# A hybrid HGRN2 and gated DeltaNet step: unread products at the start, other first transfers, one triangular inverse per head, one set of decays, eight passes of the planner

## The chip, the cores and the metric

The kernel runs on one core of a Trainium2 chip. The metric is the device time of one execution in microseconds (us), as the median of several runs. Engines are named as in the profile: PE (TensorE), PEld (its weight loads), DVE (VectorE), ACT (ScalarE), POOL (GpSimd), SP (SyncE, which here issues every DMA; SPq is its queue).

## The reference

One layer of a decoder works on 2048 prompt tokens and 8 sample tokens of width 1024, all in fp32. The mixer, cut to what matters:

```python
p = einsum('btd,de->bte', rmsnorm(x, norm_w), w_in)      # 1024 -> 4104
hq, hf, hi, hz, gq, gk, gv, gz, gb, ga = split(p)        # 8 blocks of 512; gb, ga: 4 each
# HGRN2, 4 heads of 128: S_t = diag(f_t) S_{t-1} + k_t v_t^T;  o_t = S_t^T q_t
# gated DeltaNet, 4 heads of 128; q, k, v after a causal convolution of width 4 and SiLU; q, k l2-normed
beta = sigmoid(gb);  g = -exp(a_log) * softplus(ga + dt_bias);  G = cumsum(g) in a chunk
L = exp(where(causal, G_t - G_s, -inf))
A = where(strict, (beta_t k_t . k_s) * L, 0) + I
u = solve(A, beta v) - solve(A, beta k exp(G)) S         # unit lower triangular
o = (q exp(G)) S + ((q k^T) * L) u
S = exp(G_last) S + (k exp(G_last - G))^T u
out = concat(rmsnorm(o_hgrn) silu(hz), rmsnorm(o_gdn) silu(gz)) @ w_out
y = rmsnorm(x + out, final_norm)
```

Both recurrences start from zero for the prompt and from given states for the sample tokens; the last states are outputs too.

## The kernel before

**Tiling.** The prompt is worked in two groups (g) of 1024 tokens, each of two sub-blocks (sb) of 512. For each group and each of 4 heads (h), the loop over `steps` projects eight column blocks of 128 (HI, HZ, HF, HQ for HGRN2, GK, GQ, GV, GZ for GDN). Weights and x are split into a rounded part and a rest (`wh`, `wl`, `xh`, `xl`), and `project` (L650) makes three products for each of 8 slices of the width: xh wh, xl wh, xh wl, of 512 columns, or of 256 and 264 in the sub-block that carries the 8 sample tokens too (`segs`, L641). They go to PSUM as `ps_pj` and are emptied by the `post` of that block on ACT and DVE. `out_proj` comes last (`ps_y`).

**The start.** `prep` (L564) loads rows of x (`xt`), sums their squares on ACT (`jk`), scales them by the norm weight `nwb` on DVE, and transposes them on PE (`ps_x`, L512); ACT takes `xh` out, DVE `xl`. `fetch_w` loads weights as `raw`, and ACT and POOL make `wh` and `wl`. Small inputs come beside them: `rows` (conv weights, norms), `ald` (`a_log` and `dt_bias`, broadcast), `wgr` (weights of the two gates), the conv state (`csr`).

**GDN, chunks of 128.** A head has 8 chunks in a group, four in each sub-block. `decays` (L856) makes two exponentials of differences of G for each sub-block: `la` (token t on the partitions, mask `mnA`) and `lt` (s on the partitions, mask `mnT`). `gq_after` (L882) multiplies k k^T by `la`, and k q^T by `lt`. The diagonal 32x32 blocks of A go through DRAM (`ad`) into `xa`, 32 blocks on 128 partitions. `substitute` (L920) inverts them in 31 steps of two DVE operations:

```python
SE.tensor_tensor(tm[:, :, :n], xa[:, j + 1:, j]..., ti[:, :, j:j + 1]..., op=ALU.mult)
SE.tensor_tensor(ti[:, :, j + 1:], ti[:, :, j + 1:], tm[:, :, :n], op=ALU.subtract)
```

The blocks return through `td` into `ut`, one tile per sub-block, and `inverse` (L953), once per sub-block, builds the inverse of each 128x128 matrix on PE: two rounds of a product of `la` and `ut` (`ps_v`), its copy by DVE (`v`), a product with the transposed `tn` (`ps_u`), and its copy into `ut`. `gdn_chain` (L988) then runs the recurrence over the chunks: `ps_ks`, `rr`, `ps_u`, the copy `uu` on ACT, `ps_s`, `po_g`.

**What sets the order.** No instruction is issued in the order in which the Python text makes it. `Model.record` (L68) keeps every instruction with an assumed cost, and `plan` (L111) is a list scheduler: `play` (L152) runs all of them forward through queues V, A, G, T and S (DVE, ACT, POOL, PE, SP), taking at each moment the ready instruction of lowest rank; `play_back` (L231) runs the result backward from its end and gives new ranks. After `PASSES` such rounds the order with the earliest end is fixed on each engine. On the chip every engine works through its order and waits by semaphores; SP issues its DMAs in its order. All operations of DVE, ACT, POOL and SP go through one helper and so have one line, L392; products are L505, transposes L512 (L404, L517 and L524 in the changed kernel).

Of the kernel before, what the change touches and what calls it, by code (L numbers as in the profile page):

```python
# [33 lines left out]
PASSES = 4  # L34
# [16 lines left out]
class Model:  # L51
# [59 lines left out]
    def plan(self):  # L111
# [26 lines left out]
        for _ in range(PASSES):  # L138
            t, order, start, held, end = self.play(rank, succ, pred)
# [12 lines left out]
    def play(self, rank, succ, pred):  # L152
# [9 lines left out]
        wire = 0.0  # L162
        narrow = False
# [16 lines left out]
        for _ in range(n):  # L180
# [223 lines left out]
def build(tc, x_prompt, x_sample, state_hgrn, state_gdn, state_gdn_conv, norm_w, w_in, hg_lb_logits,  # L404
# [10 lines left out]
    with ctx:  # L415
# [99 lines left out]

        def ctile(shape, name, dt=F32):
            return const.tile(shape, dt, name=name)  # L517
# [123 lines left out]
        def segs(g, sb, part=None):  # L641
            if g == 0 and sb == 0:
# [30 lines left out]
        def gates(g, xs, gt_):  # L673
# [4 lines left out]
            for sb in range(NSB):  # L678
# [13 lines left out]
                n5 = 5 if (g == 0 and sb == 0) else 4  # L692
# [11 lines left out]
        def gates_post(g, gt, out):  # L704
# [45 lines left out]
            A.activation(eG, Gc, AF.Exp)  # L750
            out.update(beta=beta, Gc=Gc, eG=eG)
# [80 lines left out]
        def gk_after(g, h, sb, gt):  # L832
            cs = slice(sb * 4, sb * 4 + 4)

            def run(u):
# [9 lines left out]
                yield  # L845
                br = small.tile([P, 4], F32, tag="br", bufs=6, name="br")
                V.tensor_tensor(br, rk, gt["beta"][:, h, cs], op=ALU.mult)
                gam = small.tile([P, 4], F32, tag="gam", bufs=6, name="gam")
                V.tensor_tensor(gam, br, rk, op=ALU.mult)
                nge = small.tile([P, 4], F32, tag="nge", bufs=6, name="nge")  # L850
                V.scalar_tensor_tensor(nge, in0=gam, scalar=-1.0, in1=gt["eG"][:, h, cs], op0=ALU.mult, op1=ALU.mult)
                V.tensor_scalar(br, br, 0.5, None, op0=ALU.mult)
                u["br"], u["nge"], u["gam"] = br, nge, gam
            return run

        def decays(g, h, sb, gt, u, prev):  # L856
# [11 lines left out]
            for key, after, mask in (("la", "ut", mnA), ("lt", "done", mnT)):  # L868
                yield from until(lambda: after in prev)
                lx = keep.tile([P, 4, P], F32, tag=key, name=key)  # L870
                for c in range(4):
                    gcol = gt["Gc"][:, h, sb * 4 + c:sb * 4 + c + 1]
                    V.scalar_tensor_tensor(lx[:, c], in0=gb4[:, c], scalar=gcol, in1=mask, op0=ALU.subtract, op1=ALU.min, reverse0=(key == "la"))
                    yield
                A.activation(lx, lx, AF.Exp)
                u[key] = lx
# [5 lines left out]
        def gq_after(sb, U):  # L882
            def run(u):
# [9 lines left out]
                la, lt, gam = u["la"], u["lt"], u["gam"]  # L893
                for c2 in range(2):
# [6 lines left out]
                    for c in range(2):  # L901
                        cc = 2 * c2 + c
                        V.scalar_tensor_tensor(la[:, cc], in0=pk[:, c, 0], scalar=gam[:, cc:cc + 1], in1=la[:, cc], op0=ALU.mult, op1=ALU.mult)
                    V.tensor_tensor(lt[:, 2 * c2:2 * c2 + 2], pk[:, :, 1], lt[:, 2 * c2:2 * c2 + 2], op=ALU.mult)
                for b in range(4):
                    Q.dma_start(U["ad"][b, sb * 4:sb * 4 + 4].rearrange("c t s -> t c s"),
# [13 lines left out]
        def substitute(U):  # L920
# [3 lines left out]
            for cg in range(4):  # L924
                Q.dma_start(xa[32 * cg:32 * cg + 32], U["ad"].rearrange("b c t s -> (b c) t s"))
# [27 lines left out]
        def inverse(u, sb):  # L953
            la, ut = u["la"], u["ut0"]
            v1, v2 = v12[sb]
            yield from hold()
            tn = btile([P, 4, P], "tn", F32)
            V.transpose(tn.rearrange("p c k -> p (c k)"), ut.rearrange("p c k -> p (c k)"))
            yield from ready(la, ut, slot=CH)
            pv = ch.tile([P, 4, 32], F32, tag="ch", name="ps_v1")  # L960
            for c in range(4):
                for q in (0, 64):
                    mm(pv[q:q + 32, c], lhsT=la[:, c, q:q + 32], rhs=ut[:, c, q + 32:q + 64], start=True, stop=True)
            for q in (0, 64):
                V.tensor_copy(v1[q:q + 32], pv[q:q + 32])
            yield from ready(v1, tn, slot=CH)
            pu = ch.tile([P, 4, 32], F32, tag="ch", name="ps_u1")
# [863 lines left out]
```

## Time and profile before

| | us |
|---|---|
| median of 3 runs | 1274.28 (1273.73 to 1276.13) |
| the profiled execution | 1279.08 |
| its span in the profile | 1277.3 |
| PE busy | 1220.3 |
| PEld, beside PE | 1056.3 |
| DVE busy | 950.4 |
| ACT busy | 519.1 |
| POOL busy | 306.3 |

The profile shows one execution. Its views are: the page with busy times per engine; windows, which give the busy time of each engine and the granted TensorE clock (PEclk, 1.00 is 2.4 GHz) in a stretch; the timeline, with each instruction's start, its duration, and in brackets the idle time of the engine before it and what ended that; waits, grouped by what the engine waited for; and lines, groups of like instructions with busy time, mean duration in ns, and idle time before them. Products are pipelined, so the duration of one is longer than the distance to the next.

### The profile page before, as it was taken

The numbers are of one execution on the slowest core, as the hardware profiler recorded it, in microseconds if no ns is written. First come the engines' busy times: TensorE is split into PE (matmuls) and PEld (weight loads), VectorE is DVE, ScalarE is ACT, GpSimd is POOL, SyncE is SP. The second block draws the span as 40 slices with busy tenths as digits, with TensorE's granted clock in tenths as the row PEclk, the third lists the DMA queues.
The fourth block names the chain that finished last, engine by engine and source line by source line (L and its number), as shares of the span: only waits on it lengthen the run. The fifth ranks groups of instructions, "written<-read, shape, count | busy, mean of one in ns | idle before, by whom it ended". The sixth has DMA issues, their size and how long they took to land.

```text
span 1277.3 us, 21956 instructions
## 1 busy us (share of the span) xinstructions
PE 1220.3 (96%) x7943; PEld 1056.3 (83%) x7943; DVE 950.4 (74%) x2419; ACT 519.1 (41%) x1533; POOL 306.3 (24%) x304
## 2 busy tenths in 40 slices
PE   3999999999999999989999999999999999999997
PEld 3988898988898889987788878888887887877785
DVE  4467897689876986888788987896788677954433
ACT  5435523643264325653365326423622464222221
POOL 5221321332232322322224213221322220001000
PEclk9999999999999999999999999999999999999998
DMA  5222532332333321334144432221332216442442
GB/s 177 66 50 85 80 41 58 71 100 64 79 93 86 92 58 42 87 108 111 34 118 57 65 68 69 70 56 30 80 76 49 68 49 202 129 144 83 144 144 82
DMA packets 144053, 107.52 MB, mean 84 GB/s; under 512 B 26122, under 2 KB 126792, under 8 KB 143928
## 3 DMA queue, kind: packets, MB, share of 16 engines
q1 hardware_dynamic: 143936, 106.02, 32.8%
q8 instruction: 65, 1.06, 0.3%
q14 instruction: 52, 0.43, 0.1%
HBM read 82.23 MB, written 23.91 MB: 83 GB/s over the span
## 4 chain that ended last, share of the span: by engine, by line
PE 69%; DVE 15%; DMA 9%; SPq 3%; issue 2%; ACT 1%; POOL 0%; POOLq 0%; DVEq 0%; ACTq 0%
PE ps_pj L505 35%; PE ps_y L505 14%; DVE tm L392 4%; DVE ti L392 4%; SPq L392 3%; PE ps_u L505 2%; PE po_h L505 2%; PE po_g L505 2%; PE ps_kq L505 2%; DMA ut<-td 2%; DMA xt<-in_x_prompt_dram 1%; DVE E L392 1%; PE ps_g L505 1%; PE ps_ks L505 1%; PE ps_hu L505 1%
## 5 line engine op out<-in xcount | busy, mean ns | idle before, releaser
L505 PE MATMUL ps_pj<-xh,wh 128*128 128x512 f32 (+2 forms) x1328 | 469.8, 354 | 7.9 <-ACT pre L392 2.7
L505 PE MATMUL ps_pj<-xh,wl 128*128 128x512 f32 (+2 forms) x1328 | 466.2, 351 | 0.0
L505 PE MATMUL ps_pj<-xl,wh 128*128 128x512 f32 (+2 forms) x1328 | 465.2, 351 | 0.2 <-DVE xl L392 0.2
L505 PEld LDWEIGHTS ps_pj<-xh,wh 128*128 128x128 f32 x1328 | 253.4, 191 | 34.8 <-ACT pre L392 3.3
L505 PEld LDWEIGHTS ps_pj<-xl,wh 128*128 128x128 f32 x1328 | 253.5, 191 | 24.2 <-DVE xl L392 0.5
L505 PEld LDWEIGHTS ps_pj<-xh,wl 128*128 128x128 f32 x1328 | 253.4, 191 | 24.3
L392 POOL TENSOR_TENSOR wl<-raw,wh 128x512 fp32r<-128x512 f32 x128 | 172.9, 1352 | 359.6 <-ACT wh L392 319.9
L392 ACT ACTIVATE wh<-raw 128x512 fp32r<-128x512 f32 x128 | 80.5, 629 | 158.4 <-PE ps_pj L505 111.3
L392 DVE TENSOR_TENSOR tm<-xa,ti 128x248 f32<-128x248 f32 (+30 forms) x248 | 107.5, 434 | 14.6 <-DMA xa<-ad 9.4
L505 PE MATMUL ps_y<-woh,oh 128*128 128x512 f32 x256 | 101.4, 400 | 4.9 <-ACT oh L392 3.0
L505 PE MATMUL ps_y<-woh,ol 128*128 128x512 f32 x256 | 101.0, 396 | 0.0
L505 PE MATMUL ps_y<-wol,oh 128*128 128x512 f32 x256 | 100.4, 394 | 0.0
L392 DVE TENSOR_TENSOR ti<-ti,tm 128x248 f32<-128x248 f32 (+30 forms) x248 | 90.4, 365 | 7.5
L392 ACT ACTIVATE jk<-xt 128x512 bf16<-128x512 f32 (+2 forms) x54 | 40.0, 740 | 121.9 <-DVE xt L392 88.2
L392 POOL TENSOR_TENSOR rso<-sso,mhalf 128x4 f32<-128x4 f32 x32 | 35.8, 1119 | 115.7 <-DVE sso L392 111.5
L505 PEld LDWEIGHTS ps_y<-woh,oh 128*128 128x128 f32 x256 | 48.5, 190 | 15.1 <-ACT oh L392 3.5
L392 POOL TENSOR_TENSOR frs<-fss,mhalf 128x1 f32<-128x1 f32 (+1 forms) x17 | 9.5, 557 | 198.4 <-DVE fss L392 180.9
L505 PEld LDWEIGHTS ps_y<-woh,ol 128*128 128x128 f32 x256 | 48.4, 189 | 10.3 <-DVE ol L392 0.4
L505 PEld LDWEIGHTS ps_y<-wol,oh 128*128 128x128 f32 x256 | 48.6, 190 | 9.4
L392 DVE TENSOR_TENSOR xt<-ps_y,xt 128x512 f32<-128x512 f32 (+1 forms) x34 | 23.4, 688 | 39.4 <-PE ps_y L505 38.0
L392 ACT ACTIVATE s_hg<-s_hg,e 128x128 f32<-128x128 f32 x80 | 32.0, 400 | 43.0 <-DVE s_hg L392 32.3
L392 DVE SCALAR_TENSOR_TENSOR s_gd<-s_gd,el,ps_s 128x128 f32<-128x128 f32 x64 | 22.1, 346 | 30.8 <-PE ps_s L505 30.3
(290 smaller groups left out, 2169.5 us busy)
## 6 DMA issues: line engine op xcount, KB each, us to landing
raw<-in_w_in_dram SPq DMA_DIRECT2D x128, 256.0 KB
xt<-in_x_prompt_dram SPq DMA_DIRECT2D x30, 512.0 KB
og_d<-sz SPq DMA_DIRECT2D x32, 256.0 KB
og<-og_d SPq DMA_DIRECT2D x32, 256.0 KB
out_dram<-xt SPq DMA_DIRECT2D x15, 512.0 KB
gb<-gate_r SPq DMA_DIRECT2D x16, 256.0 KB
out_dram<-S SPq DMA_DIRECT2D x8, 512.0 KB
xa<-ad SPq DMA_DIRECT2D x32, 128.0 KB
```

Source lines behind the costliest of these rows:

```text
L392: r = fn(*args, **kw)
L505: r = T.matmul(out, lhsT=lhsT, rhs=rhs, start=start, stop=stop)
```

## The change

It has these parts. **Start:** `warm` writes 60 products of the identity with itself (256 columns, bf16) into `po_w`, which nothing reads. The rows of the sample tokens move from sub-block 0 to sub-block 1 (`segs`, `gates`, the decode steps), so that the first sub-block is all prompt and its projections have 512 columns from step to step; the gate weights, the conv state of the samples and its copy are loaded at step 6. **One set of decays:** `la` has no mask and no exponential of its own; it is k k^T times `lt`, so A is held transposed with its column factor `gam` applied to the result, as the scale of `uu`. `eG` changes its sign once. **Joint inverses:** `ut` holds 8 chunks, `inverse` works on all of a head's group at once, and `xa` is read along its rows. **Planner:** 8 rounds in place of 4; after the first, a DMA is not put earlier than 30 us (`AHEAD`) before the rank that the backward run gave it, and (`LANES`) a DMA may not be issued before the end of the eighth one before it.

```diff
-PASSES = 4
+PASSES = 8
+WARM = 60
+AHEAD = 30.0
+LANES = 8
...
             if not left[i]:
-                heapq.heappush(soon[recs[i][0]], (0.0, i))
+                if timed and recs[i][0] == "S":
+                    ready[i] = max(0.0, rank[i] - AHEAD)
+                heapq.heappush(soon[recs[i][0]], (ready[i], i))
...
                 wire += 0.8 * late
+                lanes.append(end)
+                if len(lanes) >= LANES:
+                    clock[k] = max(clock[k], lanes[-LANES])
...
+                if timed and recs[j][0] == "S":
+                    ready[j] = max(ready[j], rank[j] - AHEAD)
...
+        def warm(n):
+
+            o = po.tile([P, 512], F32, tag="po", bufs=2, name="po_w")
+            one = ident.bitcast(BF16)
+            for _ in range(n):
+                r = T.matmul(o[:, 0:2 * P], lhsT=one[:, 0:P], rhs=one, start=True, stop=True)
+                m.queue("T", r)
+                m.record("T", r, (0.2, 0.17, False), [o], [ident])
...
+        warm(WARM)
...
-            if g == 0 and sb == 0:
+            if g == 0 and sb == NSB - 1:
                 s = [(0, 256, 0), (256, 256, NS)]
...
             A.activation(eG, Gc, AF.Exp)
+            V.tensor_scalar(eG, eG, -1.0, None, op0=ALU.mult)
...
-            for key, after, mask in (("la", "ut", mnA), ("lt", "done", mnT)):
...
+            lt = keep.tile([P, 4, P], F32, tag="lt", name="lt")
+            for c in range(4):
+                gcol = gt["Gc"][:, h, sb * 4 + c:sb * 4 + c + 1]
+                V.scalar_tensor_tensor(lt[:, c], in0=gb4[:, c], scalar=gcol, in1=mnT, op0=ALU.subtract, op1=ALU.min)
+                yield
+            A.activation(lt, lt, AF.Exp)
...
-                        V.scalar_tensor_tensor(la[:, cc], in0=pk[:, c, 0], scalar=gam[:, cc:cc + 1], in1=la[:, cc], op0=ALU.mult, op1=ALU.mult)
+                        V.scalar_tensor_tensor(la[:, cc], in0=pk[:, c, 0], scalar=gam[:, cc:cc + 1], in1=lt[:, cc], op0=ALU.mult, op1=ALU.mult)
...
-                SE.tensor_tensor(tm[:, :, :n], xa[:, j + 1:, j].unsqueeze(1).broadcast_to(sh),
+                SE.tensor_tensor(tm[:, :, :n], xa[:, j, j + 1:].unsqueeze(1).broadcast_to(sh),
...
-            for sb in range(NSB):
-                ut = keep.tile([P, 4, P], F32, tag="ut", name="ut")
-                G.memset(ut, 0.0)
-                for b in range(4):
-                    Q.dma_start(ut[32 * b:32 * b + 32, :, 32 * b:32 * b + 32],
-                                      td[b, sb * 4:sb * 4 + 4].rearrange("c s t -> s c t"))
-                U[sb]["ut0"] = ut
-            for sb in range(NSB):
-                start(inverse(U[sb], sb), 0)
...
+            ut = keep.tile([P, 8, P], F32, tag="ut", bufs=1, name="ut")
+            G.memset(ut, 0.0)
+            for b in range(4):
+                Q.dma_start(ut[32 * b:32 * b + 32, :, 32 * b:32 * b + 32], td[b].rearrange("c s t -> s c t"))
+            start(inverse(U, ut), 0)
+
+        def inverse(U, ut):
...
+            tn = btile([P, 8, 64], "tn", F32)
+            tq = dec.tile([P, 8, 32], F32, tag="tm", name="tq")
+            V.transpose(tn, ut[:, :, 0:64])
+            V.transpose(tq, ut[:, :, 64:96])
+            yield from ready(U[1]["la"], tn, tq, slot=CH)
+            pv = ch.tile([P, 8, 32], F32, tag="ch", name="ps_v1")
+            for c in range(8):
+                mm(pv[0:32, c], lhsT=la(c)[:, 32:64], rhs=tn[:, c, 0:32], start=True, stop=True)
+                mm(pv[64:96, c], lhsT=la(c)[:, 96:128], rhs=tq[:, c], start=True, stop=True)
...
-                    A.copy(uu, p2)
+                    A.activation(uu, p2, AF.Copy, scale=u["gam"][:, c:c + 1])
...
-        open_x(xs, 0, x_all, 512 + NS)
-        open_x(xs, 1, x_all)
-        first = x_rows(0) + [(0, 4, x_sample.rearrange("b t d -> (b t) d"))] + x_rows(512)
+        open_x(xs, 0, x_all)
+        open_x(xs, 1, x_all, 512 + NS)
+        first = x_rows(0) + x_rows(512) + [(1, 4, x_sample.rearrange("b t d -> (b t) d"))]
...
+            if i == 6:
+                start(sample_state())
+                start(gate_weights())
+                Q.dma_start(o_conv_s[0, :, 0:2], state_gdn_conv[0, :, 1:3])
```

**Order on SP at the start.** Before (`xt` rows of x, `nwb` the norm weight, `raw` weights):

```order
L392 DMA xt<-in_x_prompt_dram 128x1024
L392 DMA nwb<-in_norm_w_dram 128x1024
L392 DMA xt<-in_x_prompt_dram 128x1024 x2
L392 DMA raw<-in_w_in_dram 128x4x128 x2
L392 DMA xt<-in_x_prompt_dram 128x512 x2
L392 DMA xt<-in_x_sample_dram 8x512
L392 DMA rows<-in_conv_w_dram 48x128
L392 DMA rows<-in_hg_lb_logits_dram 8x128
L392 DMA rows<-in_hg_out_norm_dram 1x128
L392 DMA rows<-in_gdn_out_norm_dram 1x128
L392 DMA xt<-in_x_sample_dram 8x512
L392 DMA out_dram<-in_state_gdn_conv_dram 8x3072
```

After:

```order
L404 DMA xt<-in_x_prompt_dram 128x1024 x2
L404 DMA nwb<-in_norm_w_dram 128x1024
L404 DMA raw<-in_w_in_dram 128x4x128 x2
L404 DMA xt<-in_x_prompt_dram 128x1024
L404 DMA xt<-in_x_prompt_dram 128x512 x3
L404 DMA rows<-in_conv_w_dram 48x128
...
L404 DMA xt<-in_x_prompt_dram 128x512
L404 DMA xt<-in_x_prompt_dram 128x1024
L404 DMA raw<-in_w_in_dram 128x4x128
L404 DMA xt<-in_x_prompt_dram 128x1024
L404 DMA raw<-in_w_in_dram 128x4x128
L404 DMA xt<-in_x_sample_dram 8x512 x2
```

A second tile of x goes ahead of `nwb`; the sample rows (8x512) stand behind the next weights, where they stood on both sides of `rows`; the copy of the conv state (`out_dram`) and, further down before, `wgr` and `ald` are no longer among the first.

**Order on ACT at the start**, from its first operations; `jk` sums squares, `xh` takes transposed rows out of PSUM. Before:

```order
L392 ACTIVATE xh<-ps_x 128x4x128 x2
L392 ACTIVATE jk,ss<-xt 8x512 x2
L392 COPY cols<-ps_rows 128x58
L392 ACTIVATE e_287<-e_287 128x8
L392 ACTIVATE xh<-ps_x 128x4x128
L392 ACTIVATE nea<-ald 128x4
L392 ACTIVATE xh<-ps_x 128x4x128
L392 COPY vc<-ps_pj 128x256
L392 ACTIVATE xh<-ps_x 128x4x128
```

After:

```order
L404 ACTIVATE wh<-raw 128x512
L404 ACTIVATE xh<-ps_x 128x4x128
L404 ACTIVATE jk,ss<-xt 128x1024
L404 ACTIVATE jk,ss<-xt 128x512 x2
L404 ACTIVATE xh<-ps_x 128x4x128
L404 ACTIVATE jk,ss<-xt 128x512
L404 COPY cols<-ps_rows 128x58
L404 ACTIVATE jk,ss<-xt 128x512
L404 ACTIVATE jk,ss<-xt 128x1024
```

The exponential `nea`, which needs `ald`, stands between two evictions before; after, it comes behind step 6. Row 1's second `xh` now stands behind the squares of the next rows. On PE, 37 of the 60 unread products stand ahead of the first transposes; the other 23 stand in groups of 1 to 5 between the first transposes and products.

**Order on PE in the first inverse.** Before, the first round (`ps_v`, one tile for each sub-block) and the second (64x64):

```order
L505 MATMUL ps_sc<-E,kp 128x128 x2
L505 MATMUL ps_v_2389<-ut,la 32x32 x8
L505 MATMUL ps_v_2415<-ut,la 32x32 x8
L505 MATMUL ps_sc<-E,kp 128x128 x2
L505 MATMUL ps_pj<-xh,wl 128x512
L505 MATMUL ps_pj<-xh,wh 128x512
L505 MATMUL ps_pj<-xl,wh 128x512
L505 MATMUL ps_u_2449<-v_706,tn 32x32 x2
L505 MATMUL ps_u_2449<-tn,v_706 32x32
...
L505 MATMUL ps_v_2493<-ut,la 64x64 x4
```

After, the second round of the joint inverse, with projections between:

```order
L517 MATMUL ps_sc<-E,kp 128x128 x3
L517 MATMUL ps_v_2484<-tn,la 64x64 x8
L517 MATMUL ps_pj<-xh,wl 128x256
L517 MATMUL ps_pj<-xh,wh 128x256
L517 MATMUL ps_pj<-xl,wh 128x256
L517 MATMUL ps_pj<-xh,wl 128x256
L517 MATMUL ps_pj<-xh,wh 128x256
L517 MATMUL ps_u_2502<-ut,v_759 64x64
L517 MATMUL ps_pj<-xl,wh 128x256
L517 MATMUL ps_u_2502<-ut,v_759 64x64 x7
```

Each round has the products of all 8 chunks in one group, and between one round and the next stand projections.

## Rows read from the trace of the kernel before

**Rows 1.** The page: span, and busy time of each engine.

```profile
span 1277.3 us, 21956 instructions
...
PE 1220.3 (96%) x7943; PEld 1056.3 (83%) x7943; DVE 950.4 (74%) x2419; ACT 519.1 (41%) x1533; POOL 306.3 (24%) x304
```

**Rows 2.** Windows: length, busy of PE PEld DVE ACT POOL, clock, DMA share, GB/s.

```profile
0.00:20.00 20.00, 6.11 (x25) 5.17 (x26) 8.80 (x25) 10.74 (x22) 12.83 (x30) 1.00 0.63 189
20.00:40.00 20.00, 13.85 (x100) 13.48 (x99) 12.43 (x26) 10.64 (x25) 6.78 (x12) 0.83 0.53 157
1268.00:1277.28 9.28, 0.00 (x0) 0.00 (x0) 2.40 (x5) 0.72 (x2) 0.55 (x1) 0.65 0.18 64
```

**Rows 3.** Timeline of PE, 0 to 42 us: start, duration, instruction, [idle before].

```profile
7.97 1.97 PE L512 MATMUL ps_x<-ident,xt 128*128 128x128 f32 x8 [7.97 <-DVE xt L392]
...
20.23 0.41 PE L505 MATMUL ps_pj<-xh,wl 128*128 128x256 f32 x1
...
21.84 0.27 PE L505 MATMUL ps_pj<-xh,wl 128*128 128x256 f32 x1
...
29.79 0.59 PE L512 MATMUL ps_x<-ident,xt 8*128 8x8 f32 x4 [4.58 <-DVE xt L392]
```

**Rows 4.** Timeline of SP's queue, 0 to 36 us.

```profile
10.99 0.22 SPq L392 DMA_DIRECT2D rows<-in_gdn_out_norm_dram  x1
15.50 0.27 SPq L392 DMA_DIRECT2D xt<-in_x_sample_dram  x1
...
17.95 0.43 SPq L392 DMA_DIRECT2D wgr<-in_w_in_dram  x1
...
23.22 1.43 SPq L392 DMA_DIRECT2D raw<-in_w_in_dram  x2
```

**Rows 5.** Timeline of ACT, 14 to 34 us.

```profile
26.31 0.20 ACT L392 ACTIVATE nea<-ald 128x4 f32<-128x4 f32 x1 [3.00 <-DMA ald<-in_gdn_a_log_dram]
```

**Rows 6.** Waits of PE: us in total, times, longest us.

```profile
PE ps_v L505 <- DMA ut<-td: 7.7, 9, 2.6
...
PE ps_pj L505 <- ACT pre L392: 2.7, 3, 1.2
...
PE ps_pj L505 <- DVE szs L392: 2.3, 1, 2.3
...
PE ps_pj L505 <- ACT vc L392: 1.7, 1, 1.7
PE ps_u L505 <- DVE v L392: 1.6, 2, 0.9
```

**Rows 7.** Timelines of SP's queue and of PE, near 200 us.

```profile
195.60 3.64 SPq L392 DMA_DIRECT2D ut<-td  x8
...
199.66 0.25 PE L505 MATMUL ps_v<-ut,la 128*32 128x32 f32 x2 [0.43 <-DMA ut<-td]
201.97 0.44 PE L505 MATMUL ps_v<-ut,la 128*32 128x32 f32 x14 [2.06 <-DMA ut<-td]
```

**Rows 8.** Windows of PE: length, busy, clock, DMA share, GB/s.

```profile
417.00:421.00 4.00, 3.93 (x19) 0.57 0.29 75
...
601.00:609.00 8.00, 6.61 (x52) 0.57 0.12 21
```

**Rows 9.** Lines of DVE: count, busy us, mean ns, idle before.

```profile
L392 DVE TENSOR_TENSOR tm<-xa,ti 128x248 f32<-128x248 f32 (+30 forms) x248 | 107.5, 434 | 14.6 <-DMA xa<-ad 9.4
L392 DVE TENSOR_TENSOR ti<-ti,tm 128x248 f32<-128x248 f32 (+30 forms) x248 | 90.4, 365 | 7.5
...
L392 DVE SCALAR_TENSOR_TENSOR la<-gb,Gc,mnA 128x128 f32<-128x128 f32 x64 | 19.7, 342 | 0.0
```

**Rows 10.** Lines of ACT: count, busy us, mean ns, idle before.

```profile
L392 ACT ACTIVATE q<-pre,cols 128x512 f32<-128x512 f32 x16 | 11.5, 721 | 0.3
...
L392 ACT ACTIVATE th<-q 128x512 f32<-128x512 f32 x16 | 10.0, 624 | 2.6 <-DVE q L392 2.4
L392 ACT ACTIVATE la<-la 128x512 f32<-128x512 f32 x16 | 10.0, 625 | 10.0 <-DVE la L392 5.6 <-PE ps_hu L505 4.4
```

More of the change, by code (lines that the diff above doesn't have):

```diff
@@ L137, in plan @@
         best = None
-        for _ in range(PASSES):
-            t, order, start, held, end = self.play(rank, succ, pred)
+        for k in range(PASSES):
+            t, order, start, held, end = self.play(rank, succ, pred, k > 0)
             if best is None or t < best[0]:
@@ L691, in gates @@
                 pt = mid.tile([P, 5, 16], F32, tag="mid", name="ps_gt")
-                n5 = 5 if (g == 0 and sb == 0) else 4
+                n5 = 5 if (g == 0 and sb == NSB - 1) else 4
                 for c in range(n5):
@@ L845, in run @@
                 yield
+                gam = small.tile([P, 4], F32, tag="gam", bufs=6, name="gam")
+                V.tensor_tensor(gam, rk, gt["beta"][:, h, cs], op=ALU.mult)
+                V.tensor_tensor(gam, gam, rk, op=ALU.mult)
                 br = small.tile([P, 4], F32, tag="br", bufs=6, name="br")
[L847 to L853, printed above, removed]
+                V.scalar_tensor_tensor(br, in0=ss, scalar=0.5, in1=rk, op0=ALU.mult, op1=ALU.mult)
+                u["br"], u["nge"], u["gam"] = br, gt["eG"][:, h, cs], gam
             return run
@@ L867, in decays @@
             u["ek"] = ek
-            for key, after, mask in (("la", "ut", mnA), ("lt", "done", mnT)):
[L869 to L876, printed above, removed]
+            yield from until(lambda: "done" in prev)
+            lt = keep.tile([P, 4, P], F32, tag="lt", name="lt")
[4 more added lines that the diff above has]
+            A.activation(lt, lt, AF.Exp)
+            u["lt"] = lt
             A.activation(gb, gb, AF.Exp)
@@ L892, in run @@
                 k2, q2 = r4(u[1]), r4(u[0])
-                la, lt, gam = u["la"], u["lt"], u["gam"]
+                yield from until(lambda: "ut" in prev)
+                la = u["la"] = keep.tile([P, 4, P], F32, tag="la", name="la")
+                lt, gam = u["lt"], u["gam"]
                 for c2 in range(2):
@@ L950, in substitute @@
-            for sb in range(NSB):
-                start(inverse(U[sb], sb), 0)
-        def inverse(u, sb):
-            la, ut = u["la"], u["ut0"]
-            v1, v2 = v12[sb]
-            yield from hold()
[L957 to L961, printed above, removed]
-                for q in (0, 64):
[L963 to L967, printed above, removed]
-            for c in range(4):
-                for q in (0, 64):
-                    mm(pu[q:q + 32, c], lhsT=tn[:, c, q:q + 32], rhs=v1[:, c], start=True, stop=True)
-                mm(pu[32:64, c], lhsT=v1[:, c], rhs=tn[:, c, 0:32], start=True, stop=True)
+            ut = keep.tile([P, 8, P], F32, tag="ut", bufs=1, name="ut")
@@ L972, in inverse @@
             for q in (0, 64):
                 V.tensor_scalar(ut[q:q + 32, :, q + 32:q + 64], pu[q:q + 32], -1.0, None, op0=ALU.mult)
-            V.tensor_scalar(tn[32:64, :, 0:32], pu[32:64], -1.0, None, op0=ALU.mult)
-            yield from ready(ut, slot=CH)
+            yield from ready(tn, slot=CH)
             pv2 = ch.tile([P, 4, 64], F32, tag="ch", name="ps_v2")
-            for c in range(4):
-                mm(pv2[:64, c], lhsT=la[:, c, 0:64], rhs=ut[:, c, 64:128], start=True, stop=True)
@@ new lines, in inverse @@
+            opened[0] -= 1
+            for q in range(2):
+                V.tensor_copy(v2[64:128, q::2], pv2[64 * q:64 * q + 64])
+            yield from ready(v2, ut, slot=CH)
+            pu2 = ch.tile([P, 4, 64], F32, tag="ch", name="ps_u2")
+            for c in range(8):
+                q = 64 * (c % 2)
+                mm(pu2[q:q + 64, c // 2], lhsT=v2[:, c], rhs=ut[:, c, 64:128], start=True, stop=True)
+            for q in range(2):
+                V.tensor_scalar(ut[0:64, q::2, 64:128], pu2[64 * q:64 * q + 64], -1.0, None, op0=ALU.mult)
@@ L988, in gdn_chain @@
+            for sb in range(NSB):
+                U[sb]["ut"] = ut[:, 4 * sb:4 * sb + 4]
         def gdn_chain(g, h, U, gt):
@@ L1176, in hgrn_chain @@
             if g == 0:
[L1177 removed]
+                start(one_at_a_time(decode_hgrn(h, U[NSB - 1])))
             if g == NG - 1:
```

51 lines of the change are left out of this document (25 added, 26 removed).

## Prediction

> **What bounds the kernel now.** I read the page first. TensorE is busy for 1220.3 of 1277.3 us, 96% [rows 1]; VectorE with 950.4 comes next. So TensorE sets the time, and the change adds 60 small products to it and takes none away: only the 57 us in which it stands idle, and the stretches at a lower clock, can be won. The windows say where the idle time lies [rows 2]: 20 - 6.11 and 20 - 13.85, 20.0 us, in the first 40; 9.3 after the last product, at 1268, which the change leaves alone; the rest, 57.0 - 20.0 - 9.3 = 27.6, is scattered over the 1228 us between.
>
> The timeline of the start shows three holes [rows 3]: nothing runs before 7.97; a first block of projections starts only at 18 (the 256-column product at 20.23 takes 0.41 us, the one at 21.84 takes 0.27: the clock is at 1.2 GHz until about 21.4, and at 2.4 after the engine has been busy since 18); then PE waits until 29.79 and the clock falls once more. SP's and ACT's timelines give the causes [rows 4, 5]: SP stands from 11 until 15.50 behind small loads, the gate weights at 17.95 go out ahead of rows that PE needs, the second block of weights is asked for only at 23.22, and ACT evicts a transposed tile after 26.31 because `nea`, ahead of it, waits 3.00 us for the 16-byte broadcasts of `ald`.
>
> For the rest I read the waits of PE [rows 6]: the inverse of GDN costs 7.7 (blocks that come back from DRAM) and 1.6; projections that wait for ACT or DVE to empty a PSUM buffer cost 2.7, 2.3 and 1.7. After some of these waits the granted clock, as a mean of the stretch, is 0.57, so near its lower level, for a few us [rows 8]: 4 x 0.43 = 1.7 us lost at 417, 8 x 0.43 = 3.4 at 601, and stretches of 4 us like the first at 202, 557 and 1076, so 10.2 in all.
>
> **The change, part by part.** The sum is made against the profiled execution, 1279.1 us (span 1277.3), which lies 4.8 over the median of 1274.3.
>
> *Start.* SP now asks for two rows of x, then the norm weight, the first weights and the other rows; sample rows, gate weights, `ald` and the conv state go behind. The hole before 29.79 (4.58 us) goes, as the three things ahead of it are gone; what is late next is the first block's second half, since ACT evicts row 1's last tile only after it has squared rows 2 and 3. The norm weight lands one load of 512 KB later, so the first transpose comes up to 1.2 us later than 7.97 (the two loads issued before it in [rows 3] are the nearest guide, an estimate). The 60 products on the identity lie where PE waits: 37 ahead of the first transpose, hidden behind the 7.97 us in which there is no data; were they not hidden, the 23 behind it would cost 23 x 256 columns at 2.4 GHz, 2.5. They should have the clock at 2.4 GHz when real work comes: 17 products and a dozen transposes ran at the lower clock in the stretches from 18 to 21.4 and from 31.7 to 35, at 0.14 us each (0.41 - 0.27) for a product, so 3 at the most. Upper bound: 20.0 - 8.0 - 1.2 + 3 = 14. Lower bound: 4.6 - 1.2 - 2.5, so about 1. I take **8**: the hole (4.6) and the clock (3) are nearly sure, and what SP gains between 11 and 15.50 pays for the later norm weight.
>
> *Inverses.* Now one inverse serves eight chunks. Of 56 products per head none goes; of the loads of `ut` 4 of 8 go. Eight issues took 3.64 us on SP, and PE began the first half at 199.66 and the second, after another wait of 2.06, at 201.97 [rows 7]: the second half waited for the later four issues. With four issues all blocks land with the first half, so the waits of second halves (2.06, and 0.9 of 1.6) go. The waits of first halves come from a substitution that ends later than planned. `tm<-xa,ti` takes 434 ns and `ti<-ti,tm` of the same sizes 365 [rows 9]; the planner books both alike. After the change `xa` is read along its row instead of down its column. If the 69 ns are the stride, 248 x 69 = 17.1 us of VectorE go, 2.1 per head, about as long as PE's waits there. So of 7.7 + 1.6 and 1.7 + 3.4 of clock (202 and 601), 14.4 in all, I take **10**. Bounds: 14 and nothing, for the joint inverse must be waited for as a whole.
>
> Two statements of the Trainium skill part here. VectorE: DVE Perf Modes, section "The TRN2 errata", gives an fp32 tensor_tensor of N elements (N + 151)/0.96 ns, with no term for a stride; by it `tm` would cost what `ti` costs already, its 69 ns would be something else and would stay, and this term would be near 5. SBUF — State Buffer, section "Door 1", says that a read pays when it leaves a 16-byte line, which the column read does at each element; by it the term is the 10 above. The two rows here differ, which speaks for the second.
>
> *Full buffers.* 64 `la<-gb` (342 ns, 19.7 us) leave VectorE [rows 9], 16 exponentials of `la` (10.0 us) leave ScalarE, and the smaller evictions of the inverse are halved in number. In exchange `uu` takes a column as scale: `q<-pre,cols` with one takes 721 ns, `th<-q` of the same size without one 624 [rows 10], so 64 x 0.097 = 6.2 us more on ScalarE, 41% busy; per chunk of the recurrence that is 0.1 us, hidden while PE has projections to run, and worth 6.2 if it had none. VectorE falls by some 19.7 + 17.1 + 5, to about 908. The waits for PSUM buffers are 2.7 + 2.3 + 1.7, with 1.7 + 1.7 of clock behind the two longest: 10.1. I take **5**. Bounds: 10 won, or 6 lost, because the order is new everywhere and new places can be planned too tight.
>
> *Nothing.* Sample rows move to the second sub-block, `eG` changes sign once, `br` and `nge` lose a few [128 x 4] operations: all on engines that aren't the bound. The wait at the output projection is not touched.
>
> Sum: 8 + 10 + 5 = 23; 1279.1 - 23 = 1256.1 for such an execution, and 4.8 less, **1251 us**, for the median.
>
> **The rivals.** *Only the start* is won: the order of some 4000 instructions is drawn anew, and new waits replace the old ones in number. For it: 27.6 us over 1228 is already little, and the planner knows neither contention nor late loads. Against: two causes above go whatever the order. 1274.3 - 8 = 1266.
>
> *All of it*: 12 + 14 + 10 = 36, so 1238. For it: the planner now counts eight loads in flight, which is what SP's stops between 11 and 15.50 look like. Against: it needs every place to be right.
>
> *Slower*: the joint inverse is waited for as a whole, at every head. Now half the recurrence can go on while the other half is inverted; afterwards nothing of the head can. If PE comes to it with no projections left, it pays what it paid at 601: 2.6 idle and 3.4 of clock, 6 us. At eight heads that is 48 in place of the 14.4 paid now: 1274.3 - 8 - 14.4 + 48 = 1300. It decides from the fourth head on (24 > 14.4 + 8), so 1276 to 1300. Against: projections stand between the rounds of the new inverse, as they did before.
>
> *The change doesn't do what it says*: the identity products and the new first transfers only fill time in which PE must wait for x in any case, and the order's new waits cost the rest. Then 1274.
>
> **How the numbers follow.** Forecast 0.52, with a range of its own from 1243 to 1259; only the start 0.20; all of it 0.13; slower 0.09; no change 0.06. The range of 8 in 10 takes in the first two and most of the third: 1234 to 1270. A measurement of this kernel can tell 0.2%, 2.5 us, from nothing. Faster by more: 0.52 + 0.20 + 0.13 = 0.85; within it 0.06; slower 0.09.
>
> **What would show it.** Right: TensorE idle for about 12 us of real work in the first 40 instead of 20.0; a granted clock of 1.0 from about 8 us on; no hole near 25 to 30; `tm` at the mean of `ti`; waits for `ut` under 4 us in all; fewer than three stretches at 0.57 after 40. Wrong: `tm` as slow as before, waits of over 2 us at one inverse after another, or a longer list of projections waiting for ACT. If TensorE's idle time after 40 stays near 27 us, only the start was won.

## The result

The changed kernel takes 1251.84 us (median of 4 runs, 1249.11 to 1256.26) against 1274.01 (4 runs): a ratio of 0.9843 [0.9814, 0.9873], 20 us (16 to 24). Ratios are given as they stand on record, with a 95% interval; they differ a little from the quotient of two medians (here 0.9826, 22 us). Measured once more beside the experiments it is 0.986 [0.9834, 0.9886]. The forecast was 1251, with a range from 1234 to 1270. The kernel before lay at 1269 to 1271 in the later comparisons, so the experiments are compared by their ratios to it; 0.001 of ratio is 1.27 us, and 0.985, between its two measurements, stands for the changed kernel.

The two profiled executions, 1279.1 and 1249.1, are 30 us apart, as the first lay 4.8 over its median and the second 2.7 under: their traces show where time went, and not how much the change is worth.

The page of the changed kernel, to be held against [rows 1]:

```profile
span 1247.3 us, 21811 instructions
...
PE 1209.9 (97%) x8003; PEld 1045.9 (84%) x8003; DVE 901.7 (72%) x2301; ACT 516.8 (41%) x1517; POOL 302.8 (24%) x292
```

TensorE is the bound as before, idle for 37 us in place of 57, while 60 products were added. VectorE lost 49 us.

The windows of the start (length, busy time of PE, PEld, DVE, ACT, POOL, clock, DMA share, GB/s), against [rows 2]:

```profile
0.00:20.00 20.00, 12.65 (x82) 10.44 (x82) 8.87 (x29) 10.77 (x23) 13.17 (x31) 0.89 0.65 217
20.00:40.00 20.00, 19.24 (x150) 17.96 (x149) 15.14 (x26) 13.28 (x30) 7.39 (x7) 0.94 0.37 111
```

TensorE stands idle for 8.1 us in place of 20.0, but unread products fill a part of that. The timeline of PE shows which, against [rows 3]:

```profile
1.58 6.05 PE L533 MATMUL po_w<-ident 128*128 128x256 bf16 x37 [1.58 <-POOL ident masks.py:199]
8.59 1.09 PE L524 MATMUL ps_x<-ident,xt 128*128 128x128 f32 x8 [0.95 <-DVE xt L404]
...
11.48 0.71 PE L533 MATMUL po_w<-ident 128*128 128x256 bf16 x5
17.00 0.33 PE L524 MATMUL ps_rows<-ident,rows 58*128 58x58 f32 x1 [4.82 <-DMA rows<-in_conv_w_dram]
...
17.85 0.42 PE L517 MATMUL ps_pj<-xh,wl 128*128 128x256 f32 x1
...
23.32 0.28 PE L517 MATMUL ps_pj<-xl,wh 128*128 128x256 f32 x1
```

The hole before 29.79 is gone. The long one is now at 17: `ps_rows` waits 4.82 us for the small loads, for which it waited 2.61 before, at about the same time:

```profile
17.49 0.33 PE L512 MATMUL ps_rows<-ident,rows 58*128 58x58 f32 x1 [2.61 <-DMA rows<-in_conv_w_dram]
```

The first eight transposes take 1.09 us, where they took 1.97 [rows 3], so the unread products did bring them the higher clock. But the product at 17.85 takes 0.42 us and that at 23.32 0.28: after 4.82 us without work the clock is at its lower level again, although 37 unread products had kept the engine busy. SP's timeline gives the cause of the wait, against [rows 4]:

```profile
6.91 2.68 SPq L404 DMA_DIRECT2D rows<-in_conv_w_dram  x1
...
13.58 0.22 SPq L404 DMA_DIRECT2D rows<-in_hg_out_norm_dram  x1
```

The first small load holds SP for 2.68 us. The last goes out only at 13.58, as SP waits 3.2 us before it for weights (`raw`) to land. Its stop before 15.50 in [rows 4], 4.3 us, ended by the profile with a landing of `raw` too, where the prediction put it down to the small loads. Projections and transposes started by 40 us, by the groups of that stretch (count, then busy us and mean ns), before and after:

```profile
L512 PE MATMUL ps_x<-ident,xt 128*128 128x128 f32 (+1 forms) x52 | 10.5, 348 | 17.1 <-DVE xt L392 17.1
L505 PE MATMUL ps_pj<-xh,wh 128*128 128x256 f32 (+1 forms) x24 | 8.1, 341 | 0.3 <-ACT xh L392 0.3
L505 PE MATMUL ps_pj<-xl,wh 128*128 128x256 f32 (+1 forms) x24 | 7.6, 327 | 0.0
L505 PE MATMUL ps_pj<-xh,wl 128*128 128x256 f32 (+1 forms) x22 | 7.0, 319 | 0.0
```

```profile
L517 PE MATMUL ps_pj<-xh,wl 128*128 128x256 f32 x33 | 10.3, 315 | 0.7 <-POOL wl L404 0.6
L517 PE MATMUL ps_pj<-xh,wh 128*128 128x256 f32 x33 | 10.3, 317 | 0.0
L517 PE MATMUL ps_pj<-xl,wh 128*128 128x256 f32 x33 | 10.2, 311 | 0.0
L524 PE MATMUL ps_x<-ident,xt 128*128 128x128 f32 (+1 forms) x66 | 9.8, 280 | 1.0 <-DVE xt L404 1.0
```

That is 99 projections against 70, and 70 transposes (these 66 and 4 of `vc`) against 52. Products start 0.12 us apart, transposes 0.11: 3.5 + 2.0, so **5.5 us** are won at the start of this execution. That of after_again, with 98 and 61, gives 4.4.

PE's waits, against [rows 6] (us in total, times, longest):

```profile
PE ps_rows L524 <- DMA rows<-in_conv_w_dram: 4.8, 1, 4.8
PE ps_v L517 <- DVE tn L404: 3.9, 2, 3.3
PE ps_pj L517 <- ACT pre L404: 2.9, 2, 2.1
PE ps_pj L517 <- DVE szs L404: 2.5, 1, 2.5
PE ps_u L517 <- DVE v L404: 2.4, 2, 1.7
...
PE ps_pj L517 <- DVE sz L404: 1.3, 1, 1.3
```

At the inverse 6.3 us are left of 9.3 (11.1 with the two small groups of `ps_v` that the prediction left out). The waits for full buffers have other places and the same sum: 2.9 + 2.5 + 1.3, 6.7, as 2.7 + 2.3 + 1.7 before. After 40 us two stretches run at a low clock, where there were five [rows 8] (length, busy, clock):

```profile
326.00:330.00 4.00, 4.00 (x51) 0.57 0.15 35
532.00:540.00 8.00, 6.79 (x43) 0.79 0.63 205
```

That is 4 x 0.43 + 8 x 0.21 = 3.4 us lost, where it was 10.2. (The execution of after_again has three such stretches, 5.1 us.)

The lines of VectorE's substitution, against [rows 9]:

```profile
L404 DVE TENSOR_TENSOR ti<-ti,tm 128x248 f32<-128x248 f32 (+30 forms) x248 | 90.7, 366 | 7.5
L404 DVE TENSOR_TENSOR tm<-xa,ti 128x248 f32<-128x248 f32 (+30 forms) x248 | 85.3, 344 | 16.9 <-DMA xa<-ad 9.0 <-DMA wor<-in_w_out_dram 2.8
```

`tm` takes 344 ns, 90 less than before, and `ti` 366 as ever. On ScalarE the scaled copy costs 101 ns more, before and after:

```profile
L392 ACT COPY uu<-ps_u 128x128 f32<-128x128 f32 x64 | 16.9, 264 | 55.7 <-PE ps_u L505 55.1
```

```profile
L404 ACT ACTIVATE uu<-ps_u,gam 128x128 f32<-128x128 f32 x64 | 23.4, 365 | 59.7 <-PE ps_u L517 59.3
```

One thing the prediction had not looked at: the second round of an inverse, 64 columns per product, on PE's timeline, where each of these fp32 products has two entries. Before, the 4 chunks of a sub-block, 8 entries:

```profile
207.45 0.68 PE L505 MATMUL ps_v<-ut,la 128*64 128x64 f32 x8
```

After, 8 chunks, 16 entries:

```profile
193.65 0.69 PE L517 MATMUL ps_v<-tn,la 128*64 128x64 f32 x16 [0.59 <-DVE tn L404]
```

16 entries take as long as 8 did. The second of two chunks writes partitions 64 to 127 of PSUM, where all wrote 0 to 63 before.

### The profile page after: what moved, and what is told of

It reads as the page before. It is cut to its first block, busy times and chain, and to the rows that moved or that the text cites. A ratio compares the mean times of both kernels' runs of the same rounds, so it can differ in the third digit from the quotient of the medians.

```text
span 1247.3 us, 21811 instructions
## 1 busy us (share of the span) xinstructions
PE 1209.9 (97%) x8003; PEld 1045.9 (84%) x8003; DVE 901.7 (72%) x2301; ACT 516.8 (41%) x1517; POOL 302.8 (24%) x292
## 4 chain that ended last, share of the span: by engine, by line
PE 81%; DMA 8%; DVE 6%; ACT 1%; SPq 1%; issue 1%; POOL 1%; POOLq 0%; DVEq 0%; ACTq 0%
PE ps_pj L517 47%; PE ps_y L517 14%; PE po_g L517 2%; PE po_h L517 2%; PE ps_kq L517 2%; PE ps_u L517 2%; DMA xt<-in_x_prompt_dram 1%; SPq L404 1%; DMA wor<-in_w_out_dram 1%; PE ps_s L517 1%; PE ps_g L517 1%; DMA raw<-in_w_in_dram 1%; PE ps_hu L517 1%; PE ps_ks L517 1%; PE ps_o L524 1%
## 5 line engine op out<-in xcount | busy, mean ns | idle before, releaser
L404 POOL TENSOR_TENSOR wl<-raw,wh 128x512 fp32r<-128x512 f32 x128 | 170.0, 1331 | 368.9 <-ACT wh L404 302.2
L404 DVE TENSOR_TENSOR tm<-xa,ti 128x248 f32<-128x248 f32 (+30 forms) x248 | 85.3, 344 | 16.9 <-DMA xa<-ad 9.0
L517 PEld LDWEIGHTS ps_y<-wol,oh 128*128 128x128 f32 x256 | 48.2, 188 | 10.2 <-DVE wol L404 0.8
L404 ACT ACTIVATE uu<-ps_u,gam 128x128 f32<-128x128 f32 x64 | 23.4, 365 | 59.7 <-PE ps_u L517 59.3
```

The source lines that it names most:

```text
L404: r = fn(*args, **kw)
L517: r = T.matmul(out, lhsT=lhsT, rhs=rhs, start=start, stop=stop)
```

## The experiments

Twelve kernels, each against the kernel before on the same chip:

| run | median us | kernel before beside it | ratio | 95% interval |
|---|---|---|---|---|
| after_again | 1253.58 | 1270.16 | 0.9860 | 0.9834 to 0.9886 |
| a_onehalf | 1259.85 | 1270.92 | 0.9898 | 0.9870 to 0.9927 |
| a_tinywarm | 1254.87 | 1270.92 | 0.9875 | 0.9851 to 0.9899 |
| a_column | 1263.43 | 1270.92 | 0.9935 | 0.9910 to 0.9959 |
| b_row | 1266.10 | 1270.92 | 0.9955 | 0.9934 to 0.9976 |
| a_neither | 1268.02 | 1269.17 | 0.9976 | 0.9958 to 0.9995 |
| a_column_told | 1249.55 | 1269.17 | 0.9847 | 0.9825 to 0.9869 |
| a_split | 1249.74 | 1270.16 | 0.9843 | 0.9815 to 0.9871 |
| a_decays | 1248.12 | 1270.16 | 0.9814 | 0.9789 to 0.9839 |
| b_start | 1283.89 | 1270.16 | 1.0109 | 1.0078 to 1.0140 |
| a_plan4 | 1256.60 | 1269.17 | 0.9909 | 0.9889 to 0.9929 |
| a_fit | 1248.12 | 1269.17 | 0.9840 | 0.9823 to 0.9858 |

Names with a_ are edits of the changed kernel, with b_ of the kernel before. In the first five of the table that aren't after_again every instruction stands where it stood, so that only what was edited differs; the others have an order drawn anew.

**after_again**, without an edit.

> The changed kernel once more, as it is, as the base for the runs beside it: a ratio of 0.982 to 0.986 to the kernel before by every theory.

0.986, at the upper end of what was expected; the two measurements of the changed kernel agree.

**a_onehalf**

```diff
...
-                q = 64 * (c % 2)
-                mm(pv2[q:q + 64, c // 2], lhsT=la(c)[:, 64:128], rhs=tn[:, c], start=True, stop=True)
+                mm(pv2[0:64, c], lhsT=la(c)[:, 64:128], rhs=tn[:, c], start=True, stop=True)
...
-                mm(pu2[q:q + 64, c // 2], lhsT=v2[:, c], rhs=ut[:, c, 64:128], start=True, stop=True)
+                mm(pu2[0:64, c], lhsT=v2[:, c], rhs=ut[:, c, 64:128], start=True, stop=True)
...
```

> The changed kernel with one thing undone: the products of the second round (ps_v2, ps_u2, 64 columns) all write partitions 0 to 63, as in the kernel before; the order on every engine is the same, and so is the number of copies. Theory A (a gain that my prediction left out: chunks that take turns between the two halves of the partitions run side by side, 31 and 35 ns apart in the changed kernel's trace against 63 and 65 before): the distance goes back to about 64 ns, 256 x 31 = 8 us, so about 1260. Rival B (the distance hangs on the new order around them, not on the partitions): the distance stays near 33 ns and the time near 1252.

The 16 entries of the first inverse on PE's timeline:

```profile
197.27 1.15 PE L517 MATMUL ps_v<-tn,la 128*64 128x64 f32 x16 [0.59 <-DVE tn L404]
```

1.15 us where the changed kernel takes 0.69. With 16 such groups that is 16 x 0.46 = 7.4 us, and the ratio says 0.0048, 6 us. The interval overlaps that of after_again a little, but the same edit made on a_column (a_neither, below) costs 0.0041, 5 us, too. Theory A: chunks that write to different halves run side by side.

**a_column** and **b_row**: one line, each way.

```diff
-                SE.tensor_tensor(tm[:, :, :n], xa[:, j, j + 1:].unsqueeze(1).broadcast_to(sh),
+                SE.tensor_tensor(tm[:, :, :n], xa[:, j + 1:, j].unsqueeze(1).broadcast_to(sh),
```

> The changed kernel with xa read down its column, as before; every engine's order is the same. It reads the other triangle of the blocks, so its values differ, not its work. Theory A (the stride costs VectorE time, and substitutions that end late are what PE waits for): tm goes from 344 ns back to about 434, 248 x 90 = 22 us of VectorE, 2.8 per head; PE's waits at the inverse grow by 1 to 2.8 at each of several heads, 1257 to 1264. Rival B (slack in the new order covers it): tm slows down, the time stays within 2 of 1252. Rival C (a VectorE operation has no term for a stride): tm stays at 344.

> The kernel before with xa read along its row; every engine's order is the same. It reads the other triangle of the blocks, so its values differ, not its work. Theory A (late substitutions): tm goes from 434 to about 344 ns, PE's wait for ut falls from 7.7 to about 3, and with the clock behind two of these waits the time falls by 5 to 9, 1265 to 1269. Rival B (the wait is that for DMA issues behind one another, whatever the substitution takes): tm falls, the waits and the time of 1274 stay.

In a_column `tm` is back at the old duration, and 0.0085, 11 us, are lost:

```profile
L404 DVE TENSOR_TENSOR tm<-xa,ti 128x248 f32<-128x248 f32 (+30 forms) x248 | 110.6, 446 | 16.8 <-DMA xa<-ad 11.7
```

But not where theory A had it. PE's waits in a_column:

```profile
PE ps_v L517 <- DVE tn L404: 4.1, 2, 3.5
PE ps_pj L517 <- ACT vc L404: 3.2, 1, 3.2
PE ps_u L517 <- DVE v L404: 2.7, 2, 2.1
...
PE ps_pj L517 <- ACT thf L404: 1.9, 2, 1.2
PE ps_kp L524 <- DVE kp L404: 1.7, 1, 1.7
```

The inverse waits 4.1 and 2.7, as with the row read (3.9 and 2.4). What is new are projections and transposes that wait for ScalarE and VectorE (`vc` 3.2, `thf` 1.9, `kp` 1.7). One place shows the chain, on ScalarE and PE:

```profile
544.50 1.06 ACT L404 ACTIVATE jk<-xt 128x1024 bf16<-128x1024 f32 x1 [3.26 <-DMA xt<-in_x_prompt_dram]
...
545.55 0.35 ACT L404 COPY vc<-ps_pj 128x256 f32<-128x256 f32 x1
```

```profile
545.96 0.58 PE L517 MATMUL ps_pj<-xh,wh 128*128 128x256 f32 x1 [3.18 <-ACT vc L404]
```

ScalarE stands 3.26 us for rows of x that landed late, the copy `vc` is queued behind them, and PE waits for its buffer; the clock then falls (0.58 us for the next product). Between the two profiled executions, 14.4 us apart, PE is idle for 7.9 us more (45.3 against 37.4) and busy for 6.5 more with the same products (1216.4 against 1209.9), at a mean granted clock of 0.986 against 0.992: the clock behind the waits costs nearly as much as the waits. Why that load is late wasn't followed; the substitution shares VectorE with the steps that free the tiles of x, which would explain it and isn't shown. In b_row `tm` falls from 434 to 326 ns, PE's wait for `ut` from 7.7 to 5.3 only, and 0.0045, 6 us, are won.

**a_neither**: both edits of a_onehalf and a_column.

> The changed kernel with both of a_onehalf and a_column: second round in one half of the partitions, xa read down its column (the other triangle, so its values differ, not its work); every engine's order is the same. Theory A (these two made nearly the whole gain, and start, joint inverse, single decays and planner come to nothing together; 7 and 12 add up): 1268 to 1273, a ratio of 0.998 or more to the kernel before. Rival B (both fill the same slack): 1262 to 1265, about 0.993. Rival C of the prediction (start and order are worth 13): 1260.

0.9976 [0.9958, 0.9995]: the two edits take 0.0126, 16 us, of the 19 away, nearly their sum (6 + 11). All else in the change is worth 1 to 5 us together, though the start is in it whole (99 projections and 68 transposes by 40 us).

**a_column_told**: a_column, and the planner books 0.10 us more for `tm`.

```diff
+                m.more = 0.1
                 SE.tensor_tensor(tm[:, :, :n], xa[:, j + 1:, j].unsqueeze(1).broadcast_to(sh),
...
+                m.more = 0.0
...
-        return 0.155 + 0.06 * scal + (0.00047 if fast else 0.00105) * n, 0.0, not psum and op != "transpose"
+        return self._m.more + 0.155 + 0.06 * scal + (0.00047 if fast else 0.00105) * n, 0.0, not psum and op != "transpose"
```

> a_column with the planner told that tm takes 0.10 us longer than it books; the order is drawn anew. Theory A (what cost 12 in a_column was not VectorE's load but an order that doesn't know of it; a_decays, with 20 us more of VectorE that the planner books, was not slower): 1250 to 1257, with few waits of projections for VectorE and ScalarE. Rival B (25 us more of work on VectorE cost this much in any order): 1261 to 1265.

Its `tm` is as slow as in a_column:

```profile
L406 DVE TENSOR_TENSOR tm<-xa,ti 128x248 f32<-128x248 f32 (+30 forms) x248 | 110.3, 445 | 21.5 <-DMA xa<-ad 16.8
```

and it runs at 0.9847, like the changed kernel itself. 25 us more on VectorE cost nothing that can be told once the order knows of them. A new draw alone does not explain it: the orders drawn here by the new planner (changed kernel, a_split, a_decays, a_column_told, a_fit) lie between 0.981 and 0.986, and a_column at 0.9935. Its waits of PE lie elsewhere, for `sz`, and hardly at the inverse:

```profile
PE ps_pj L519 <- DVE sz L406: 7.7, 3, 3.1
...
PE ps_v L519 <- DVE tn L406: 1.2, 2, 0.7
```

The expected "few waits for VectorE" was wrong; they are as many, but the time is theory A's.

**a_split**: one inverse per four chunks; `ut` and its four loads stay joint.

```diff
...
-            start(inverse(U, ut), 0)
+            for sb in range(NSB):
+                start(inverse(U, ut, sb), 0)
...
-            for c in range(8):
+            for c in range(4):
...
```

> The changed kernel with the inverse split again, four chunks each, the four loads of ut still joint. Theory A of the prediction (one inverse for eight chunks saves waits of second halves): waits of ps_v and ps_u come up to 8 or more from 6.3, some 5 us more of VectorE in small copies, 1254 to 1258. Rival B (a joint inverse must be waited for as a whole, half a recurrence could go on earlier): 1246 to 1250. Rival C (only the joint loads mattered): 1252 within 2.

0.9843: rival C. PE's waits for `tn` and `v` are 0.9 and 0.7, less than in the joint inverse, and others take their place. Joining the rounds brought nothing that can be told, and waiting for the whole cost nothing.

**a_decays**: the second set, made and not used.

```diff
...
+            for key, after, mask in (("la", "ut", mnA), ("lt", "done", mnT)):
...
-                la = u["la"] = keep.tile([P, 4, P], F32, tag="la", name="la")
-                lt, gam = u["lt"], u["gam"]
+                la, lt, gam = u["la"], u["lt"], u["gam"]
...
```

> The changed kernel with the second set of decays made again as before (mask, 64 VectorE operations, 16 exponentials) and overwritten unread. Theory A (VectorE's load is what projections wait for when their buffers are full; a_column, with 25 us more of VectorE, lost 12 there): 19.7 us more of VectorE and 10 of ScalarE cost 6 to 10, 1258 to 1262, in waits of ps_pj for ACT and DVE. Rival B (they fit beside PE's work, as they lie early in a head): 1252 within 2.

The operations are there again:

```profile
L404 DVE SCALAR_TENSOR_TENSOR la<-gb,Gc,mnA 128x128 f32<-128x128 f32 x64 | 20.1, 361 | 0.1
```

and the kernel is not slower: 0.9814, 5 us under the changed kernel, with intervals that overlap a little. Theory A falls, as its cost is not there. Rival B is right that the work fits, though the time is below what it said; added work can't have made it so, and what is left is the new order, which by itself moves the time by some us.

**a_tinywarm**

```diff
-                r = T.matmul(o[:, 0:2 * P], lhsT=one[:, 0:P], rhs=one, start=True, stop=True)
+                r = T.matmul(o[:, 0:16], lhsT=one[:, 0:P], rhs=one[:, 0:16], start=True, stop=True)
```

> The changed kernel with its 60 unread products cut from 256 to 16 columns, at the same places in the same order: they keep nothing busy for long. Theory A of the prediction (they bring the clock, worth up to 3): the first transposes go back from 1.1 to 2.0 us for eight, and the time is 2 to 3 us longer, 1255. Rival B (the clock falls anyway while PE waits for the small rows until 17, and products at 17.6 to 20 already take 0.41 us; the 8 unread products after 19.99 stand in the way of real ones for 2 us): the first projection still starts at about 17, and the time is 0 to 2 us shorter, 1250 to 1252.

PE's timeline:

```profile
9.31 1.97 PE L524 MATMUL ps_x<-ident,xt 128*128 128x128 f32 x8 [6.57 <-DVE xt L404]
...
17.21 0.31 PE L524 MATMUL ps_rows<-ident,rows 58*128 58x58 f32 x1 [3.68 <-DMA rows<-in_conv_w_dram]
...
17.83 0.41 PE L517 MATMUL ps_pj<-xl,wh 128*128 128x256 f32 x1
```

The first transposes do run at the lower clock, and the first projections start as late as with the unread products (17.45 and 17.26), for the small loads. 98 projections and 66 transposes have started by 40 us against 99 and 70. The time is 0.9875, whose interval overlaps those of the changed kernel: a gain of some 3 us by the unread products is neither shown nor excluded, and the count at 40 us shows next to none.

**b_start**: start alone, on the kernel before (`warm`, `segs`, order of `first`, step 6, as in the change).

> The kernel before with the start alone: unread products, sample rows in the second sub-block, gate weights and conv state at step 6; its planner, inverses and decays as they were. Theory A (the start is worth what is lost less by 40 us, 5.8, and the parts add up): about 1268, PE's hole of 4.6 near 25 to 30 gone. Rival B (without eight loads in flight in the planner's model the first transfers are no better): the hole or one like it stays, 1274. Rival C (an order drawn anew moves the rest by as much): the first 40 us gain, the time doesn't.

1.0109: slower than before by 14 us. By 40 us 82 projections have started (before 70, changed kernel 99), with 52 transposes as before, so 12 x 0.12 = 1.4 us are won there. The rest is lost later, in an order drawn anew: rival C, and far larger than thought; PE waits 2.7 for `sz`, 2.7 for `vc`, 2.8 for `pre` and 6.2 for `ut`. What of that comes from the edits and what from the draw wasn't parted.

**a_plan4**

```diff
...
-PASSES = 8
+PASSES = 4
...
-            t, order, start, held, end = self.play(rank, succ, pred, k > 0)
+            t, order, start, held, end = self.play(rank, succ, pred)
...
```

> The changed kernel with the planner of before: four rounds, no bound on early DMAs, no count of eight in flight. Theory A (the planner's rules for DMAs and its further rounds are worth 5 or more, which b_start, 14 slower with the old planner, points to): 1258 or more, with DMA waits of PE that the changed kernel doesn't have. Rival B (orders drawn anew differ by 5 either way, without a rule behind it): 1248 to 1257.

0.9909, 7 us slower than the changed kernel, by theory A, but in one place. SP's queue and PE at the start:

```profile
3.24 5.21 SPq L395 DMA_DIRECT2D xt<-in_x_prompt_dram  x4
8.49 0.92 SPq L395 DMA_DIRECT2D nwb<-in_norm_w_dram  x1
```

```profile
1.59 9.26 PE L524 MATMUL po_w<-ident 128*128 128x256 bf16 x60 [1.59 <-POOL ident masks.py:199]
19.28 3.67 PE L515 MATMUL ps_x<-ident,xt 128*128 128x128 f32 x16 [8.44 <-DVE xt L395]
...
27.88 0.58 PE L508 MATMUL ps_pj<-xh,wh 128*128 128x256 f32 x1 [4.63 <-ACT xh L395]
```

The norm weight goes out at 8.49, behind nine loads of x and weights, and the first transposes run at 19.28 in place of 8.59. By 40 us 64 projections and 40 transposes are done, 35 and 30 fewer: 4.2 + 3.3 = 7.5 us, as much as the whole difference. Which of the planner's three edits does it wasn't tried. Nor is it a rule of the old planner: in b_start, which has it too, the norm weight goes out first of all, at 0.81.

**a_fit**: the changed kernel with 0.06 us more booked for `tm` and `ti` (the edit of a_column_told with that number for both, and xa read along its row).

> The changed kernel with the planner told that tm and ti take 0.06 us longer than it books (their measured means are 344 and 366 ns, the booked ones average 289); the order is drawn anew. Theory A (an order that knows how long the substitution takes has no wait behind it): the waits of ps_v for tn and of ps_u for v (6.3 in all) go, and the clock behind them, 1244 to 1249. Rival B (other waits take their place): 1250 to 1256.

```profile
PE ps_x L526 <- DVE ss L406: 2.6, 1, 2.6
PE ps_v L519 <- DVE tn L406: 2.4, 2, 2.2
...
```

The waits at the inverse fall to 2.4 + 0 and others come up (`ps_x` with 2.6): rival B in the waits, though the time is theory A's. 0.9840, 1248.12 us: it is 2 to 3 us under after_again by ratio, within the noise. No version here beats the changed kernel clearly; a_decays and a_fit, 1248.1 both, are the fastest measured.

## Why the prediction was right, and where not

The time was right, and so was the first step: TensorE is the bound, and its idle time, with the clock behind it, is what can be won. The terms of the sum came out otherwise.

*Start*, forecast 8: 5.5 or 4.4 by the count at 40 us, of which a_neither leaves at most 5. The right part was the hole before 29.79. Three sentences failed. "They should have the clock at 2.4 GHz when real work comes": the first transposes have it, but the engine stands still again from 12 to 17, and products at 17.6 to 20 take 0.42 us with and without the unread ones (a_tinywarm). The words "what is late next is the first block's second half" named the wrong thing: it is the small loads ahead of the whole block. And "what SP gains between 11 and 15.50" was little: it still stands 3.2 us there for a landing of `raw`. The 1.2 us for the norm weight rest on no row ([rows 3] has no loads); the first transpose came 0.62 later, at 8.59. The sign for the start that the text gave, a clock of 1.0 from 8 us on, was not met (0.89, 0.94). It was a poor sign: [rows 2] has 1.00 for 0 to 20, where a product of [rows 3] takes 0.41 us.

*Inverses*, forecast 10: the size of the stride was right and even short (69 ns forecast, 90 measured, 102 in the same order), but the step "the waits of first halves come from a substitution that ends later than planned" named too small a place. Undoing the stride leaves the waits at the inverse as they are and makes projections wait instead; it costs 11 us in this order and nothing measurable in an order that books it. The joint inverse itself, with its fewer waits of second halves, is worth nothing that a_split can tell. By the rows alone the term looks nearly met, with 3.0 us of waits gone and 3.4 of clock (326 is left of 202 and 601); but a_neither has the smaller waits as well (3.9 and 1.8), and hardly any gain.

Of the two statements weighed there the measurement decides. An fp32 `tensor_tensor` costs more down a column, 446 ns against 344 in the same order. The Trainium skill, VectorE: DVE Perf Modes, section "The TRN2 errata", has no term for it: for 208 elements its formula makes 374 ns, an estimate that fits the read along the row (376 in the changed kernel) and not that down the column (542 in a_column); SBUF — State Buffer, section "Door 1", which has one for reads that leave a 16-byte line, agrees.

*"Of 56 products per head none goes"* was costed at nothing, and is the term that was missing: the products stay, and the second round takes half the time, 6 to 7 us, because the new layout writes two halves of the partitions by turns. The order shown ahead of the prediction names these products but not the partitions they write; the changed kernel has `q = 64 * (c % 2)` for them.

*Full buffers*, forecast 5: nothing in the waits, and at most 1.7 of clock (534 is left of 417 and 557). The waits are 6.7 before and after, and work that leaves VectorE earlier in a head brings no time (a_decays). `uu`, forecast at 97 ns more each, takes 101 more, hidden as said.

*The planner* had no term of its own. With the old one the change came out 7 us slower (a_plan4), by the count at 40 us through the norm weight that its order put late. What the new planner is worth by itself stays open.

So the account that the runs bear out is: second round 6 and stride 11, 16 together, and 1 to 5 for all else, in which the start is the one part with a count behind it, against the 20 (16 to 24) measured. The first 16 are shown with every instruction in its place; the split of the rest is argued. The rival on the slower side, a joint inverse that is waited for at every head, is not there: 6.3 us in all. That the sum, 8 + 10 + 5 = 23, came out near was in part luck: its third term brought next to nothing, its second came on another path, and a term of 6 to 7 was missing.

## What to carry to other kernels

Where a planner fixes the order, an operation that takes longer than it books can cost time even on an engine that isn't the bound. Here 25 us of VectorE that the planner hadn't booked cost 11, and nothing measurable once booked: compare booked and measured durations first, before removing work. A layout that lets short products write different partition halves in turn was worth 6 to 7 us here, and is worth trying in other chains of 64-column products. And experiments that keep every instruction in its place tell causes apart; an edit that redraws the order also moves the time through the draw: it fell by 5 us in a_decays, where work was only added (with intervals that overlap), and rose by 14 in b_start, where draw and edits weren't parted.

## What was not expected of the hardware

Products of 64 columns on partitions 0 to 63 and 64 to 127 in turn run side by side: 16 entries in 0.69 us against 1.15 in one half, in fp32, with nothing asked for but the output's partitions. In the changed kernel's trace two of them start 5 to 7 ns apart and the next two 58 ns behind; in a_onehalf each starts 58 ns behind the one before. The Trainium skill, TensorEngine Tiling (Array Packing), section "Key Properties", says that tiles of the array work independently; these starts agree with that, and no run here shows how the array was divided. And a VectorE read down a column of a 32x32 block of fp32 takes 30% longer than along its row (446 against 344 ns in the mean of 8 to 248 elements).
